# Another order for the first stage of a hybrid decoder block, and other PSUM banks for its first three projections

## The chip, the cores and the metric

The kernel runs on one core of a Trainium2 chip. The metric is the time of one execution on the device in microseconds, the median of three runs. The trace is that of one profiled execution. The engines are TensorE (PE, with its weight loads PEld), VectorE (DVE), ScalarE (ACT), GpSimd (POOL) and SyncE (SP), which issues the DMA transfers.

## The reference, cut to what matters

One decoder block over 512 tokens of 1024 values, all in float32:

```
h = RMSNorm(x)
P = h @ W_in            # q, k, v of two attentions, their branch gates, two merge gates
y_A = sliding-window attention with sinks(q, k, v) @ W_up_A
y_B = gated sum of compressed, selected and window attention @ W_up_B
x = x + (sigmoid(gA) * y_A + sigmoid(gB) * y_B) @ W_out
x = x + ConvFFN(RMSNorm(x));  out = RMSNorm(x)
```

## The kernel before, in words

Every float32 product is made of three matmuls of shorter operands: each matrix is split into a high part (rounded) and a low part (the rest), and high x high, high x low and low x high are summed in one PSUM bank (`three`, lines 108 to 112). The split is a cast on ScalarE (`split`, line 93) and a subtraction on VectorE or GpSimd (line 99).

The kernel has four stages. The first one takes `x` and the first weights and makes the values `v` and the first three projections. Attention follows, in units of one block of 128 queries and one group of heads; between the steps of a unit the later projections, the gates and the up-projections are issued as fillers, so that TensorE has work while the softmax runs on VectorE and ScalarE. Then come the output projection and the FFN with its convolution, which are nearly all matmuls.

The first stage is written as a list of short units, `FIRST` (lines 37 to 45), which are issued one by one in just that order (`do`, line 183) under a manual schedule: each engine executes its own units in the order of the list and waits at a unit whose inputs are not there. The units that matter here:

- `tpTH`: four transposes of token block T, half H of `x` into a bank of the tag `pt`; `xhTH` (ScalarE, line 207) and `xlTH` (VectorE, line 209) take the high and low part out of it, to `XH` and `XL`.
- `vTHCI`: two matmuls (line 237) of the values of token block T into the bank of `vT`. The banks are `mm`, `mm`, `o` and `sc` for T = 0 to 3. `vbT`, `vaT` (ScalarE) and `lbT`, `laT` (VectorE, line 183) read them when the sum is complete, `egT` and `gT` the gates.
- `ms`, `r` (GpSimd, line 217), `dg`, `rb`, `rs`: the reciprocal norms of the rows, and their copy over all columns.
- `jgJ` (VectorE, line 262), `jhJ` (ScalarE, line 265), `jlJ` (GpSimd, line 269): weight block J of the first three projections, scaled and split. J = 0, 1, 2 are `ka`, `qa0`, `qa1`.
- `pJK`: three matmuls of projection J, row block K, straight from `XH` and `XL`; `mJ` multiplies the result by the norms (line 277).
- `xaK` (GpSimd, line 283), `scK`, `yhK`, `ylK` (lines 285, 291, 293): the normalised `x`, which the later projections read as `xTh` and `xTl`.

PSUM has eight banks here, by tag: `mm` 2, `sc` 2, `pt` 3, `o` 1. A new tile of a tag takes the bank of the oldest one and so waits for the readers of it. Behind the list a scheduler orders the rest of the program on each engine by times that it works out itself, starting from the state in which the first stage leaves the engines; the first projection there is `kc`, whose result is cut into blocks (`cx`, line 390, and `XX0`) for the hidden layer `h1_00` (line 405).

Of the kernel before, what the change touches and what calls it, by code (L numbers as in the profile page):

```python
# [34 lines left out]


FIRST = '''
dum1 sq00 gt gc tp00 wh1 dum2 wh0 wl1 dum3 xh00 wl0 tp10 sq10 xl00 v0000 v0001 xh10 v0002 wh2 v1000 xl10 tp20 wh3 wl2
v1002 sq20 v1010 wl3 v0012 xh20 v1011 sq30 v0011 xl20 v2000 v2001 sq01 v2010 tp30 wh5 v0010 wh4 wl5 v1012 xh30 wl4
v1001 tp01 sq11 xl30 v3001 tp11 xa3 xh01 v3002 sq21 xl01 tp21 v0101 xh11 tc xa2 v0102 tp31 xh21 xl11 v1100 wh7 v1101  # L40
xl21 xa1 xh31 v1102 wl7 v0100 sq31 pg xl31 wh6 xa0 ms jg0 v1110 pgc r v0112 wl6 v1112 xa4 v3100 dg v0111 jh0 nr v1111
jg1 v0110 xa6 eg1 v2110 vb1 v2111 eg0 g1 vb0 rb jh1 g0 jl0 v3111 lb0 v2011 rs lb1 v2002 jg2 va1 v2100 va0 v2012 v2102
v2112 sc3 jh2 v2101 jl1 sc0 v3012 v3011 eg2 sc2 yh0 v3101 g2 v3010 vb2 v3110 va2 la0 yh3 v3000 la2 v3102 la1 yh2 v3112
yl3 jl2 p04 lb2 eg3 vb3 g3 p00 va3 la3 p02 lb3 sc6 p07 yl0 yh6 p01 xa7 yl2 p06 yl6 p05 xa5 sc7 p03 sc1 yh7 p22 sc4 yh1
p20 sc5 yh4 m0 p23 yh5 yl7 p26 yl5 p24 yl1 p25 yl4 p27 p21 p11 m2 p17 p16 p14 p13 p15 p10 p12 m1'''
NPA, NPB = (1, 2, 3), (2, 3)
BANKS = dict(mm=2, sc=2, pt=3, o=1)
SPLIT, CUT = 3, 256
# [15 lines left out]
def hybrid(tc, x, wv, wblk, w1, w2, wua, wub, wout, wfi, wfo, nmix, nffn, nfin, sinks, par, table, onehot, out):  # L64
# [9 lines left out]
    with es:  # L74
# [9 lines left out]
        def slot(i, shape, dt, name):  # L84
            return SL.tile(shape, dt, tag=f"s{i}", name=name)

        def bank(tag, name):
            return PS.tile([P, 512], F32, tag=tag, name=name, bufs=BANKS[tag])

        f = lambda t: t.bitcast(F32)  # L90
# [18 lines left out]
        def three(ps, wh, wl, xh, xl, start, stop):  # L109
            T.matmul(ps, wh, xh, start=start, stop=False)  # L110
            T.matmul(ps, wh, xl, start=False, stop=False)  # L111
            T.matmul(ps, wl, xh, start=False, stop=stop)  # L112
# [25 lines left out]
        def rstd_of(ssq, name):  # L138
            r = SM.tile([P, 1], F32, tag="rstd", bufs=3, name=f"rstd_{name}")
            V.tensor_scalar(r, ssq, 1.0 / D, EPS, op0=ALU.mult, op1=ALU.add)  # L140
            G.tensor_tensor(r, r, mhalf, op=ALU.pow)
            return r
# [22 lines left out]
        diag, rs = (AT.tile([P, S], F32, tag=g, name=n) for g, n in (("ptl", "diag"), ("pth", "rs")))  # L165
        scale, rstd, nrstd, *sq2 = (SM.tile([P, NT], F32, tag=g, name=g + "x", bufs=2) for g in ("nma", "sma", "nmb", "smb", "nmc"))
        first = FIRST.split()
        ps_v, out_v, tp_x, psj, raws, hls, sums, pgs_t, tot, last_of = {}, {}, {}, {}, {}, {}, {}, [], [], {}
        early = AORD.split()[:3]
# [3 lines left out]
        def out_of(t):  # L173
            if t not in out_v:
                ps = ps_v[t][:, 0:384].rearrange("p (n d) -> p n d", d=64)
                out_v[t] = ps[:, 0:2], ps[:, 2:6], SM.tile([P, 24], F32, tag="eg", name=f"eg{t}", bufs=2)
            return out_v[t]

        def values(dst, t, part, hi):
            if hi:  # L180
                A.mul(dst[:, t, :, 0:64], part, rstd[:, t : t + 1])
            else:
                V.scalar_tensor_tensor(dst[:, t, :, 64:128], part, rstd[:, t : t + 1], f(dst[:, t, :, 0:64]), op0=ALU.mult, op1=ALU.subtract)

        def do(u):
# [44 lines left out]
            elif what == "wl":  # L230
                V.scalar_tensor_tensor(xu(wvl, n[0]), xu(wvr, n[0]), gcol[:, n[0] : n[0] + 1], f(xu(wvh, n[0])), op0=ALU.mult, op1=ALU.subtract)
            elif what == "v":
                t, h, c, i = n
                if t not in ps_v:
                    ps_v[t] = bank(("mm", "mm", "o", "sc")[t], f"v{t}")
                for k in range(4 * h + 2 * c, 4 * h + 2 * c + 2):
                    T.matmul(ps_v[t][:, :NV], xu((XH, XH, XL)[i], k)[:, t * P : (t + 1) * P], xu((wvh, wvl, wvh)[i], k),
                             start=(u == mine[0] and k % 2 == 0), stop=(u == mine[-1] and k % 2 == 1))
            elif what in ("va", "la"):
                values(VA, n[0], out_of(n[0])[0], what == "va")  # L240
            elif what in ("vb", "lb"):
                values(VB, n[0], out_of(n[0])[1], what == "vb")
            elif what == "eg":
                A.activation(out_of(n[0])[2], ps_v[n[0]][:, 384:408], AF.Exp, scale=nrstd[:, n[0] : n[0] + 1])
            elif what == "g":
                t, eg = n[0], out_of(n[0])[2]
                V.tensor_scalar(eg, eg, 1.0, None, op0=ALU.add)
                V.reciprocal(gate[:, t].rearrange("p a h -> p h a"), eg.rearrange("p (h a) -> p h a", a=3))
                if t == 0:
                    V.tensor_scalar(gate[:, 0, 0], gate[:, 0, 0], valid0, None, op0=ALU.mult)  # L250
            elif what == "tc":
                V.tensor_copy(tabc, tab.rearrange("p (b h) -> p b h", b=2)[:, :, None].to_broadcast([33, 2, 16, 8]))
            elif what == "pg":
                pgs_t.extend(bank("pt", f"pg{i}") for i in range(2))
                for c0, c1, b, i, d0 in pgs:
                    T.matmul(pgs_t[i][:, d0 : d0 + c1 - c0], tabc[:, b].rearrange("p c h -> p (c h)"), oh[:, c0:c1], start=True, stop=True)
            elif what == "pgc":
                for c0, c1, b, i, d0 in pgs:
                    A.copy(gsb[:, c0:c1], pgs_t[i][:, d0 : d0 + c1 - c0])
            elif what == "jg":  # L260
                w = raws[n[0]].rearrange("p (k q) -> p k q", k=KD)
                V.tensor_tensor(w, w, gcol[:, :, None].to_broadcast([P, KD, P]), op=ALU.mult)
            elif what == "jh":
                hls[n[0]] = WR.tile([P, 2, 1024], F32R, tag="hl", name=f"hl_{early[n[0]]}", bufs=3)
                A.copy(hls[n[0]][:, 0], raws[n[0]])
            elif what == "jl":
                for c in range(0, 1024, 256):
                    cs = slice(c, c + 256)
                    G.tensor_tensor(hls[n[0]][:, 1, cs], raws[n[0]][:, cs], f(hls[n[0]])[:, 0, cs], op=ALU.subtract)
            elif what == "p":  # L270
                j, k = n
                if j not in psj:
                    psj[j] = bank(("mm", "mm", "sc")[j], f"p_{early[j]}")
                ks = slice(k * P, (k + 1) * P)
                three(psj[j], hls[j][:, 0, ks], hls[j][:, 1, ks], xu(XH, k), xu(XL, k), u == mine[0], u == mine[-1])
            elif what == "m":
                V.tensor_tensor(psj[n[0]], psj[n[0]], rs, op=ALU.mult)
            elif what == "xa":
                k = n[0]
                sums[k] = AT.tile([P, S], F32, tag="P", name=f"xa{k}", bufs=8)  # L280
                for c in range(0, S, 256):
                    cs = slice(c, c + 256)
                    G.tensor_tensor(sums[k][:, cs], f(xu(XH, k))[:, cs], f(xu(XL, k))[:, cs], op=ALU.add)
            elif what == "sc":
                V.scalar_tensor_tensor(sums[n[0]], sums[n[0]], gcol[:, n[0] : n[0] + 1], rs, op0=ALU.mult, op1=ALU.mult)
            elif what in ("yh", "yl"):
                if not xTh:
                    xTh.extend(slot(h, [P, 4, S], F32R, f"xTh{h}") for h in range(2))
                    xTl.extend(slot(2 + h, [P, 4, S], F32R, f"xTl{h}") for h in range(2))
# [523 lines left out]
        for mp in range(4):  # L813
            hl = weight(wub[mp], f"up1_{mp}", G if mp in U1J else None)
            for mm in range(2):
# [6 lines left out]
                gt = GB[m // 4][:, m % 4]  # L822
# [24 lines left out]
        for t in range(NT):  # L847
# [14 lines left out]
            r = rstd_of(ssq, f"n2_{t}")  # L862
# [43 lines left out]
        for h in range(2):  # L906
# [10 lines left out]
            for t in range(NT):  # L917
# [91 lines left out]
```

## Time and profile before

| | us |
|---|---|
| median of three runs | 758.54 |
| the runs | 758.47 to 760.33 |
| the profiled execution | 759.33 |
| its span | 757.5 |

The span is what the engines' instructions cover; the execution's own time is 1.8 us longer. In the rows below a line of a timeline is: start, duration of the group, engine, line of the kernel, operation, output<-inputs, shapes, count; in brackets the idle time of the engine ahead of it and what the profile thinks ended it. Numbers of tiles are left out there (`hl_qa` is that of `qa0`, `qa1` and others).

### The profile page before, as it was taken

To read this page: it belongs to the slowest core of one execution; us is meant where nothing else is said; L and a number is where in the kernel's file an instruction comes from. 1 tells how busy PE (TensorE), PEld (TensorE's weight loads), DVE (VectorE), ACT (ScalarE), POOL (GpSimd) and SP (SyncE) were. 2 spreads that over 40 slices of the span, in tenths; PEclk is the share of its full clock that TensorE was granted. 3 is DMA by queue.
4 is the path that set the end of the run, shared out by engine and by line. 5 is a ranking of instruction groups with operands and counts; after the bars stand their busy time and mean duration, and the time that the engine had idled before them with its cause. 6 is when DMAs were issued, how large, how long until landed. Compare 5 with 4: busy or idle time off the path is not lost.

```text
span 757.5 us, 9971 instructions
## 1 busy us (share of the span) xinstructions
PE 741.2 (98%) x3600; PEld 621.3 (82%) x3600; DVE 447.5 (59%) x915; ACT 375.6 (50%) x699; POOL 198.1 (26%) x275
## 2 busy tenths in 40 slices
PE   9899999999999999999999999999999999999996
PEld 7788887788888888878899888888888888888885
DVE  5987888457554667857466565556556654214223
ACT  7556778555657674664245344434444443113213
POOL 3973867425442554407200000000000000002001
PEclk9999999999999999999999999999999999999999
DMA  8353356221111211406222322222232324323202
GB/s 309 126 127 112 111 165 171 84 83 58 56 57 57 83 57 56 141 28 199 79 84 84 105 91 98 97 96 100 89 106 88 106 88 135 104 91 98 97 29 111
DMA packets 26029, 76.75 MB, mean 101 GB/s; under 512 B 3923, under 2 KB 6107, under 8 KB 25980
## 3 DMA queue, kind: packets, MB, share of 16 engines
q1 hardware_dynamic: 25964, 76.12, 30.9%
q8 instruction: 28, 0.46, 0.2%
q14 instruction: 21, 0.17, 0.1%
q10 hardware_dynamic: 16, 0.00, 0.0%
HBM read 72.96 MB, written 3.15 MB: 100 GB/s over the span
## 4 chain that ended last, share of the span: by engine, by line
PE 86%; DVE 5%; ACT 4%; issue 2%; POOL 1%; DMA 1%; SPq 0%; POOLq 0%; ACTq 0%; DVEq 0%
PE ug L112 11%; PE ug L110 11%; PE ug L111 11%; PE fo L902 5%; PE fo L904 5%; PE fo L903 5%; PE pT L592 2%; PE up L110 2%; PE p_ga L111 2%; PE p_ga L110 2%; PE up L112 2%; PE p_ga L112 2%; PE up L111 2%; PE wo L112 2%; PE wo L110 2%; PE wo L111 2%
## 5 line engine op out<-in xcount | busy, mean ns | idle before, releaser
L111 PE MATMUL ug<-hTl,hl_fi 128*128 128x512 f32 (+1 forms) x376 | 141.1, 375 | 0.0
L112 PE MATMUL ug<-hTh,hl_fi 128*128 128x512 f32 (+1 forms) x376 | 141.1, 375 | 0.0
L110 PE MATMUL ug<-hTh,hl_fi 128*128 128x512 f32 (+1 forms) x376 | 140.9, 376 | 0.0
L928 POOL TENSOR_TENSOR X<-X,nfin 128x512 f32<-128x512 f32 x4 | 5.2, 1314 | 296.9 <-ACT junk L926 296.9
L885 ACT ACTIVATE cv<-ug,prm 128x512 f32<-128x512 f32 x44 | 34.4, 781 | 96.2 <-PE ug L112 96.2
L111 PEld LDWEIGHTS ug<-hTl,hl_fi 128*128 128x128 f32 x376 | 70.8, 188 | 12.9
L112 PEld LDWEIGHTS ug<-hTh,hl_fi 128*128 128x128 f32 x376 | 70.8, 188 | 12.7
L110 PEld LDWEIGHTS ug<-hTh,hl_fi 128*128 128x128 f32 x376 | 70.6, 188 | 12.7
L886 DVE SCALAR_TENSOR_TENSOR cv<-ug,prm,cv 128x511 f32<-128x511 f32 x44 | 33.0, 750 | 77.0 <-ACT cv L885 76.9
L903 PE MATMUL fo<-hl_fo,AH 128*128 128x512 f32 x176 | 68.5, 389 | 0.0
L902 PE MATMUL fo<-hl_fo,AH 128*128 128x512 f32 x176 | 67.3, 389 | 0.0
L99 DVE TENSOR_TENSOR hl_fo<-raw_fo,hl_fo 128x1024 fp32r<-128x1024 f32 x22 | 27.1, 1234 | 64.6 <-ACT hl_fo L93 64.6
L93 ACT CAST hl_fo<-raw_fo 128x1024 fp32r<-128x1024 f32 x22 | 23.1, 1052 | 65.7 <-PE fo L904 65.7
L99 DVE TENSOR_TENSOR hl_fi<-raw_fi,hl_fi 128x1024 fp32r<-128x1024 f32 x44 | 53.5, 1217 | 0.8 <-ACT hl_fi L93 0.8
L904 PE MATMUL fo<-hl_fo,AL 128*128 128x512 f32 x128 | 49.8, 389 | 0.0
L522 ACT ACTIVATE Pb<-Pb,nmb 128x512 f32<-128x512 f32 (+3 forms) x64 | 35.9, 562 | 27.5 <-DVE nmb L585 26.1
L93 ACT CAST hl_fi<-raw_fi 128x1024 fp32r<-128x1024 f32 x44 | 45.6, 1039 | 1.5 <-PE wo L112 1.5
L99 DVE TENSOR_TENSOR ptl<-pT,pth 128x512 fp32r<-128x512 f32 x54 | 36.5, 684 | 15.0 <-ACT pth L93 11.3
L93 ACT CAST pth<-pT 128x512 fp32r<-128x512 f32 x54 | 30.8, 585 | 22.4 <-PE pT L592 14.6
L585 DVE CUSTOM_DVE_ANT_0 Pb<-scores,TB 128x512 f32<-128x512 f32 (+3 forms) x64 | 30.6, 485 | 16.8 <-PE scores L581 15.7
L902 PEld LDWEIGHTS fo<-hl_fo,AH 128*128 128x128 f32 x176 | 33.0, 188 | 6.9
L903 PEld LDWEIGHTS fo<-hl_fo,AH 128*128 128x128 f32 x176 | 33.0, 188 | 6.9
(335 smaller groups left out, 1769.4 us busy)
## 6 DMA issues: line engine op xcount, KB each, us to landing
raw_fi<-in_wfi_dram SPq DMA_DIRECT2D x44, 512.0 KB, 3.2
raw_fo<-in_wfo_dram SPq DMA_DIRECT2D x22, 512.0 KB, 3.2
raw_w<-in_w_dram SPq DMA_DIRECT2D x8, 512.0 KB, 3.3
raw_ga<-in_wblk_dram SPq DMA_DIRECT2D x8, 512.0 KB, 3.5
raw_gb<-in_wblk_dram SPq DMA_DIRECT2D x8, 512.0 KB, 3.3
raw_wo<-in_wout_dram SPq DMA_DIRECT2D x5, 512.0 KB, 4.1
x<-in_x_dram SPq DMA_DIRECT2D x8, 256.0 KB, 5.7
raw_qa<-in_wblk_dram SPq DMA_DIRECT2D x4, 512.0 KB, 5.0
```

The costliest lines, as they stand in the source:

```text
L93: A.copy(hi, src)
L99: (eng or V).tensor_tensor(lo[sl], src[sl], f(hi)[sl], op=ALU.subtract)
L110: T.matmul(ps, wh, xh, start=start, stop=False)
L111: T.matmul(ps, wh, xl, start=False, stop=False)
L112: T.matmul(ps, wl, xh, start=False, stop=stop)
L522: last_exp[0] = A.activation(a[0], a[1], AF.Exp, **k)
L585: V.tensor_tensor_reduce(ptile[:, :n], ps[:, :n], Tt[:, h, y0 : y0 + n], 1.0, HUGE, ALU.add, ALU.min, nm)
L885: A.activation(c, ps, AF.Identity, scale=cw(2, blk), bias=cb(blk))
L886: V.scalar_tensor_tensor(c[:, 1:], ps[:, : S - 1], cw(1, blk), c[:, 1:], op0=ALU.mult, op1=ALU.add)
L902: T.matmul(po[t], ah, wh, start=(k == 0), stop=False)
L903: T.matmul(po[t], ah, wl, start=False, stop=False)
L904: T.matmul(po[t], al, wh, start=False, stop=(k == NF - 1))
```

## The change

The list `FIRST` is replaced by another order of the same units, and the banks of the three projections `p` now have the tag `pt` in place of `mm`, `mm` and `sc`:

```diff
 FIRST = '''
-dum1 sq00 gt gc tp00 wh1 dum2 wh0 wl1 dum3 xh00 wl0 tp10 sq10 xl00 v0000 v0001 xh10 v0002 wh2 v1000 xl10 tp20 wh3 wl2
...
+dum1 sq00 gt gc tp00 wh1 dum2 xh00 wl1 dum3 wh0 xl00 tp10 sq10 v0000 wl0 v0002 wh2 v0001 wh3 wl2 tp20 sq20 v0010 wl3
...
             elif what == "p":
                 j, k = n
                 if j not in psj:
-                    psj[j] = bank(("mm", "mm", "sc")[j], f"p_{early[j]}")
+                    psj[j] = bank("pt", f"p_{early[j]}")
```

TensorE around the first product of `p_ka`, before: all of `v` is done when it comes (`v3_247` is the bank of `v3`).

```order
L237 MATMUL v3_247<-wvl1_85,XH1_91 128x408 x2
L237 MATMUL v3_247<-wvh0_82,XH0_90 128x408 x2
L237 MATMUL v3_247<-wvh1_83,XH1_91 128x408 x2
L237 MATMUL v3_247<-wvh0_82,XH0_90 128x408 x2
L237 MATMUL v3_247<-wvh1_83,XL1_93 128x408 x4
L110 MATMUL p_ka_434<-XH1_91,hl_ka_332 128x512
L111 MATMUL p_ka_434<-XL1_93,hl_ka_332 128x512
```

The same place now:

```order
L237 MATMUL v2_227<-wvl1_85,XH1_91 128x408 x2
L237 MATMUL v3_231<-wvl0_84,XH0_90 128x408 x2
L237 MATMUL v3_231<-wvh0_82,XH0_90 128x408 x2
L225 MATMUL rb_366<-diag_97,VA_95 128x512
L110 MATMUL p_ka_376<-XH1_91,hl_ka_321 128x512
L111 MATMUL p_ka_376<-XL1_93,hl_ka_321 128x512
```

And TensorE in the third projection of the list, `p_qa0`, now:

```order
L110 MATMUL p_qa0_467<-XH1_91,hl_qa0_345 128x512
L111 MATMUL p_qa0_467<-XL1_93,hl_qa0_345 128x512
L112 MATMUL p_qa0_467<-XH1_91,hl_qa0_345 128x512
L237 MATMUL v2_227<-wvh1_83,XH1_91 128x408 x2
L110 MATMUL p_qa0_467<-XH1_91,hl_qa0_345 128x512
L111 MATMUL p_qa0_467<-XL1_93,hl_qa0_345 128x512
L112 MATMUL p_qa0_467<-XH1_91,hl_qa0_345 128x512
L237 MATMUL v3_231<-wvh1_83,XL1_93 128x408 x2
L237 MATMUL v2_227<-wvh0_82,XL0_92 128x408 x2
```

The last products of `v2` and `v3`, ten pairs, moved from ahead of the first projection into the third; `rb` stands right ahead of `p_ka`.

VectorE ahead of and at the blocks of `p_kc`, which the hidden layer `h1_00` reads as `XX0`, before:

```order
L467 SCALAR_TENSOR_TENSOR QA0_559<-p_qa1_482,QA0_559 64x512
L467 SCALAR_TENSOR_TENSOR QA0_559<-p_qa0_517,QA0_559 64x512
L390 TENSOR_TENSOR cx_545<-p_kc_609,prm_88 64x8x31 x3
L585 ISA Pa_588,nma_586<-scores_589,TA_575 128x130
L585 ISA nma_586 128x1
L390 TENSOR_TENSOR cx_545<-p_kc_609,prm_88 64x8x31 x2
L585 ISA Pa_613,nma_586<-scores_614,TA_575 128x130
L585 ISA nma_586 128x1
L390 TENSOR_TENSOR cx_545<-p_kc_609,prm_88 64x8x31 x3
L99 TENSOR_TENSOR XX0_687<-cx_545,XX0_687 128x16x62
```

The same place now:

```order
L183 SCALAR_TENSOR_TENSOR VA_95<-v2_227,smax_100,VA_95 128x2x64
L183 SCALAR_TENSOR_TENSOR VB_89<-v2_227,smax_100,VB_89 128x4x64
L183 SCALAR_TENSOR_TENSOR VB_89<-v3_231,smax_100,VB_89 128x4x64
L277 TENSOR_TENSOR p_qa0_467<-p_qa0_467,rs_98 128x512
L457 TENSOR_TENSOR KA_549<-p_ka_376,KA_549 64x4x128
L458 TENSOR_TENSOR KA_549<-p_ka_376,KA_549 64x4x128
L467 SCALAR_TENSOR_TENSOR QA0_559<-p_qa1_428,QA0_559 64x512
L467 SCALAR_TENSOR_TENSOR QA0_559<-p_qa0_467,QA0_559 64x512
L390 TENSOR_TENSOR cx_545<-p_kc_609,prm_88 64x8x31 x8
L467 SCALAR_TENSOR_TENSOR QA0_559<-p_qa0_467,QA0_559 64x512
L99 TENSOR_TENSOR XX0_687<-cx_545,XX0_687 128x16x62
```

The first reductions of `scores` moved behind `XX0`, and the last readers of `v2` and `v3` (`VA`, `VB`) moved to just ahead of it. On TensorE the two first pairs of `scores` moved likewise, from between `p_kc` and `p_qa2` to behind both.

TensorE near the end of attention, from the fourth pair of `scores` of a window unit (`scores_3413` is the first of the next unit's; `ob` is an attention output, `up0` and `up1` are fillers), before:

```order
L580 MATMUL scores_3413<-KS_1281,QB1_1971 128x160
L581 MATMUL scores_3413<-KS_1281,QB1_1971 128x160
L110 MATMUL up0_6_3399<-YA1_1057,hl_up0_3_3327 128x512
L111 MATMUL up0_6_3399<-YA1_1057,hl_up0_3_3327 128x512
L112 MATMUL up0_6_3399<-YA1_1057,hl_up0_3_3327 128x512
L739 MATMUL ob_3276<-pch_3283,VZ_547 128x128
L739 MATMUL ob_3276<-pcl_3284,VZ_547 128x128
```

The same place now:

```order
L111 MATMUL up1_3_3676<-YB0_1985,hl_up1_1_3653 128x512
L112 MATMUL up1_3_3676<-YB0_1985,hl_up1_1_3653 128x512
L580 MATMUL scores_3413<-KS_1281,QB1_1971 128x160
L581 MATMUL scores_3413<-KS_1281,QB1_1971 128x160
L592 MATMUL pT_3374<-ident_87,Pb_3107 128x128
L592 MATMUL pT_3374<-ident_87,Pb_3136 128x128
L592 MATMUL pT_3374<-ident_87,Pb_3173 128x128
L592 MATMUL pT_3374<-ident_87,Pb_3205 128x128
L580 MATMUL scores_3444<-KS_1281,QB1_1971 128x160
```

The end of `up0_6`, all of `up0_7` and the first six matmuls of `up1_3` moved ahead of `scores_3413`.

## Rows read from the trace of the kernel before

**Rows 1.** The page: busy time and instructions by engine, clock by slices.
```profile
PE 741.2 (98%) x3600; PEld 621.3 (82%) x3600; DVE 447.5 (59%) x915; ACT 375.6 (50%) x699; POOL 198.1 (26%) x275
...
PEclk9999999999999999999999999999999999999999
```

**Rows 2.** TensorE's waits at 0-60, 60-160, 300-420 us: us, times, longest.
```profile
PE p_ka L110 <- ACT xTh L291: 2.8, 1, 2.8
...
PE scores L580 <- DVE nma L585: 1.0, 2, 0.7
...
PE p_qb L110 <- ACT cx L409: 0.6, 1, 0.6
...
PE p_ksl L110 <- DVE cx L390: 0.2, 1, 0.2
...
PE up L110 <- DVE oy L606: 1.6, 1, 1.6
PE up L110 <- DVE nmb L585: 0.2, 1, 0.2
```

**Rows 3.** Busy time by engine from 130 to 300 us (length, then each engine, clock).
```profile
130.00:300.00 170.00, 169.78 (x882) 142.50 (x881) 102.06 (x332) 103.54 (x229) 76.14 (x107) 1.00 0.19 63
```

**Rows 4.** Timeline of TensorE around the first projection.
```profile
29.32 1.28 PE L237 MATMUL v<-wvh,XH 128*128 128x408 f32 x6
30.44 0.91 PE L237 MATMUL v<-wvh,XL 128*128 128x408 f32 x4
34.13 0.76 PE L110 MATMUL p_ka<-XH,hl_ka 128*128 128x512 f32 x1 [2.79 <-ACT xTh L291]
...
37.53 0.40 PE L112 MATMUL p_ka<-XH,hl_ka 128*128 128x512 f32 x1
...
41.17 0.39 PE L110 MATMUL p_qa<-XH,hl_qa 128*128 128x512 f32 x1
```

**Rows 5.** Busy time in stretches: length, PE, PEld, DVE, ACT, POOL, granted clock.
```profile
30.00:40.00 10.00, 7.21 (x27) 5.76 (x26) 9.93 (x19) 4.40 (x11) 10.00 (x12) 0.83 0.69 173
...
20.00:56.34 36.34, 33.55 (x147) 28.27 (x146) 33.52 (x52) 20.20 (x38) 31.57 (x39) 0.95 0.47 131
```

**Rows 6.** Timeline of VectorE: the readers of `v` ahead of `p_ka`.
```profile
33.73 0.77 DVE L183 SCALAR_TENSOR_TENSOR VA<-v,smax,VA 128x128 fp32r<-128x128 f32 x3
```

**Rows 7.** Timeline of GpSimd behind `r`.
```profile
20.02 1.95 POOL L217 TENSOR_TENSOR smax<-nmax,warm 128x4 f32<-128x4 f32 x1
21.94 4.32 POOL L283 TENSOR_TENSOR xa<-XH,XL 128x256 f32<-128x256 f32 x4
26.22 3.81 POOL L269 TENSOR_TENSOR hl_ka<-raw_ka,hl_ka 128x256 fp32r<-128x256 f32 x4
...
37.31 4.62 POOL L283 TENSOR_TENSOR xa<-XH,XL 128x256 f32<-128x256 f32 x4
...
46.21 3.96 POOL L99 TENSOR_TENSOR hl_kc<-raw_kc,hl_kc 128x256 fp32r<-128x256 f32 x4 [1.56 <-issue]
50.13 2.83 POOL L99 TENSOR_TENSOR hl_qa<-raw_qa,hl_qa 128x256 fp32r<-128x256 f32 x4
```

**Rows 8.** Timeline of TensorE: the start of `p_kc`.
```profile
52.05 0.39 PE L110 MATMUL p_kc<-xTh,hl_kc 128*128 128x512 f32 x1
```

**Rows 9.** The blocks of `p_kc` (line 390, durations in ns), their cast and low part.
```profile
L390 DVE TENSOR_TENSOR cx<-p_kc,prm x8: 399/411/419, 57.7 to 61.2; 64x248 f32<-64x248 f32 x8
...
61.63 1.03 ACT L93 CAST XX<-cx 128x992 fp32r<-128x992 f32 x1 [0.72 <-DVE cx L390]
...
62.69 1.19 DVE L99 TENSOR_TENSOR XX<-cx,XX 128x992 fp32r<-128x992 f32 x1 [1.10 <-ACT XX L93]
```

**Rows 10.** Busy time from `scores_3413` to `up1_1`: all engines, then line 536 alone (VectorE).
```profile
305.41:318.15 12.74, 12.47 (x75) 10.45 (x73) 10.13 (x41) 7.10 (x22) 8.09 (x12) 1.00 0.63 197
...
305.41:318.15 12.74, 1.36 (x2) 1.00 0.63 197
```

**Rows 11.** Timeline of TensorE: the wait for the last attention output.
```profile
328.38 0.47 PE L110 MATMUL up<-YB,hl_up 128*128 128x512 f32 x1 [1.65 <-DVE oy L606]
```

More of the change, by code (lines that the diff above doesn't have):

```diff
@@ L37 @@
 FIRST = '''
-dum1 sq00 gt gc tp00 wh1 dum2 wh0 wl1 dum3 xh00 wl0 tp10 sq10 xl00 v0000 v0001 xh10 v0002 wh2 v1000 xl10 tp20 wh3 wl2
[L39 to L45, printed above, removed]
+dum1 sq00 gt gc tp00 wh1 dum2 xh00 wl1 dum3 wh0 xl00 tp10 sq10 v0000 wl0 v0002 wh2 v0001 wh3 wl2 tp20 sq20 v0010 wl3
+v0012 xh10 tp30 v0011 sq30 xl10 v1011 v1000 xh30 v1002 v1001 xh20 xl30 v1010 wh5 v2000 xl20 v3002 wh4 v2001 wl5 xa3
+sq01 v2010 wl4 v3000 wh6 tp01 v1012 sq11 wl6 tp11 xa0 v2012 xh01 tp21 tc sq21 v0101 v0100 xl01 xh11 xa1 v2011 v3012
+xh21 xl11 v1100 wh7 v1101 xl21 v0102 sq31 v0110 xa2 jg0 v1110 tp31 v1102 wl7 xh31 pg jh0 ms jg1 r v0111 pgc v3111 jl0
+v2111 dg v0112 v1112 jh1 nr v1111 xl31 v2112 eg1 jg2 v2101 eg0 v3001 vb0 v3010 vb1 rb g0 va0 xa6 va1 p04 lb0 jh2 la0
+p03 la1 lb1 rs jl2 p00 g1 p02 sc2 p07 p01 sc0 yh2 p05 sc3 yh0 p06 xa5 yl2 yh3 p22 p26 yl3 p23 jl1 sc6 p24 yl0 yh6 p25
+p21 yl6 p27 m0 p20 xa4 sc5 p17 m2 yh5 v2100 p14 sc1 xa7 v3102 v2002 yl5 yh1 v2110 v3100 yl1 p16 v3101 sc7 v3110 v3112
+sc4 yh7 p12 v3011 yl7 yh4 p13 va3 yl4 v2102 eg3 vb3 p11 la3 vb2 p15 g3 eg2 va2 p10 g2 la2 lb2 lb3 m1'''
 NPA, NPB = (1, 2, 3), (2, 3)
```

## The prediction

> **What bounds the kernel now.** I read the page first: TensorE is busy 741.2 us [rows 1] of a span of 757.5 us. Whatever an edit does elsewhere counts only where TensorE waits, or where its clock falls. So the second view was the list of what TensorE waited for, by stretches [rows 2]. Up to 60 us there is one wait in the middle, 2.8 us before the first projection `p_ka`; from 60 to 160 us there are some 3 us in small waits on VectorE and ScalarE; from 300 to 420 us there are 1.8 us, of which 1.6 us stand where the last attention output is awaited. From 130 to 300 us it hardly waits at all: 169.78 us busy of 170 [rows 3].
>
> Third, the timeline of TensorE around the wait in the middle [rows 4]. The last product of `v` ends at 31.35 us and `p_ka` begins at 34.13 us. After the wait the matmuls start 0.43 us apart (eight of them from 34.13 to 37.53 us) and from there 0.2275 us apart (16 of them from 37.53 to 41.17 us). The stretch 30 to 40 us has a granted clock of 0.83 [rows 5]: TensorE ran at the lower of its levels, 1.2 GHz, after that idle time. It cost 3.40 us for what takes 8 x 0.2275 = 1.82 us at 2.4 GHz, so 1.58 us more. The idle times of 1.65 us and less [rows 2, 11] show no such fall, the clock stays at 9 tenths or more in all 40 slices of the page [rows 1].
>
> What ended the wait is named ScalarE's `xTh`. By the program it was another thing: `p_ka` takes the bank of `v0`, and the last reader of `v0` is VectorE's `la0`, first of three on line 183 that start at 33.73 us [rows 6]. It ends just ahead of 34.13. It stands late in VectorE's queue, which was busy 33.52 of the 36.34 us from 20 us on [rows 5].
>
> **The change part by part.** The units are the same; none is added or dropped. What differs is the order, and the banks of `p`.
>
> *The wait before `p_ka`.* The bank of `p_ka` is now one of the transposes', whose last reader is `xl31`. In the new order that stands a few units before, well ahead of `la0`. Ten pairs of `v` products (0.37 us a pair, three from 29.32 to 30.44 us) now stand behind the first projections, so `p_ka` comes up at about 31.35 - 3.7 = 27.6 us. It needs `hl_ka`, whose high part needs `jg0` and `jh0` alone and whose low part is GpSimd's first work behind `r` (end 21.97 us, then 3.81 us, so 25.8 us [rows 7]). So the whole 2.79 us goes, and with it the fall of the clock: 2.79 + 1.58 = 4.37 us. What is late next is GpSimd: `jl0`, `xa6`, `jl2`, `xa5`, `jl1` behind `r` are 3 x 3.81 + 2 x 2.16 = 15.75 us by [rows 7], so 37.7 us; the first product of `p_qa0`, 16 units of 0.68 us behind the start of `p_ka`, is at 27.6 + 10.9 = 38.5 us. I count no wait there, with 0.8 us to spare.
>
> *The place behind `p_kc`.* With 4.37 us gained `p_kc` starts at 52.05 - 4.37 = 47.68 us [rows 8]. In the new order `p_kc` and `p_qa2` come in a piece, 48 matmuls or 10.92 us, then two short pairs of `scores` (130 columns, an estimated 0.3 us by their share of 512), then `h1_00`: TensorE is there at 58.9 us. `h1_00` needs `XX0`, and VectorE's queue has to come through: its work of 33.52 us from 20 us on [rows 5], then the eight blocks of `cx` (0.41 us each, 3.3 us), ScalarE's cast (1.03 us) and the low part (1.19 us) [rows 9], so 20 + 33.52 + 3.3 + 1.03 + 1.19 = 59.0 us if VectorE never waits. It waited 2.8 us in that time before (36.34 - 33.52), and with all of that it would be 61.8 us. The wait is between 0.1 and 2.9 us; I take 1.0, nearer to the low end, since part of the waits before were for projections that now come earlier.
>
> *From 60 to 95 us.* The waits there are VectorE's and ScalarE's pace: 1.0 us for `nma` and 0.6 and 0.2 us for `cx` [rows 2]. A TensorE that arrives earlier waits longer for the same readers. Between 0 and as much again (1.8 us), I take 0.6.
>
> *The end of attention.* The scheduler places everything behind the first stage, and starting from another state it places the fillers otherwise. In the old order 21 filler matmuls (three of `up0_6`, twelve of `up0_7`, six of `up1_3`) stand between `scores_3413` and `up1_1`; in the new order none, they all stand ahead. The old stretch lasted from 305.41 to 318.15 us, 12.74 us. Without the fillers (21 x 0.2275 = 4.78 us) and without the 0.3 us that TensorE waited, its own work there is 7.66 us. VectorE was busy 10.13 us there, of which 1.36 us are products of gates (line 536) that go ahead with the fillers [rows 10]: 8.77 us remain. So TensorE waits at least 1.1 us, were VectorE packed without a gap, and 3.7 us if VectorE keeps the 2.6 us of gaps it had. I take 2.2. The 1.65 us at the very end [rows 11] I leave as they are.
>
> The sum: 4.37 - 1.0 - 0.6 - 2.2 = 0.57 us gained. The profiled execution took 759.33 us (its span of 757.5 and 1.8 around it), which gives 758.8. The median of the runs is 758.54, 0.8 below the profiled one, which gives 758.0. By the bounds the terms reach from 4.37 - 0.1 - 1.1 = 3.2 us gained to 4.37 - 2.9 - 1.8 - 3.7 = 4.0 us lost; they will not all be at one end, and the forecast's own range is 756.3 to 760.2.
>
> **The rivals.**
>
> *The gain is kept.* The softmax at the end may be packed well enough that TensorE's lead simply moves everything forward, as the stretch without waits from 130 to 300 us suggests [rows 3]. For it: VectorE too starts the later stages earlier, and ScalarE is busy only 7.10 of the 12.74 us [rows 10]. Against it: with no filler in that stretch TensorE has less to do (7.66 us) than VectorE (8.77 us). Time: 758.54 - 4.37 + 0.3 for a small wait at `h1_00`, 754.5 us.
>
> *The end of attention eats more than the lead.* One place, the stretch from `scores_3413` to `up1_1`: if the fillers hid all they covered, their 4.78 us turn into waiting. Then 4.37 - 1.0 - 0.6 - 4.78 = -2.0, so 760.5 us; and if one of these idle times is as long as the 2.79 us of [rows 4] the clock falls once more and 1.58 us come on top, 762.1 us. I put it at 761.3. It decides from 2.8 us of waiting there, where the lead is used up, and is slower by more than a measurement can tell from 5.0 us. For it: 2.6 us of gaps in VectorE in the same stretch. Against it: 0.8 us of them were waits for fillers that now come first.
>
> *GpSimd becomes the bound of the first stage.* The new order has its chain from `r` to `jl1` with hardly a gap, beside VectorE's products of two inputs. In the trace the low part of a block costs 3.96 us on GpSimd while VectorE works on such products and 2.83 us a little later [rows 7], and the halves of `xa` cost 1.155 us (4 in 4.62 us) at their longest. Sixteen pieces at 1.155 us are 18.5 us and end at 40.5 us, 2.0 us behind what `p_qa0` needs. Time: 758.0 + 2.0 = 760.0 us. The Trainium skill, page "GPSIMD Engine Reference", section "1. Specifications", states that GpSimd shares its SBUF interfaces with VectorE and contends with VectorE instructions that have two SBUF inputs. By that rule the denser order would be paid for on GpSimd; the trace agrees in direction, 3.96 against 2.83 us for the same work.
>
> *The change doesn't do what it says.* `p_ka` could wait as long as before, on another reader of the transposes' banks (`pgc` for the two next) or on `hl_ka`. Against it: these end by 26 us by the rows above. Then no lead arises, and only the worse placed end counts: 758.54 + 1.1 = 759.6 us.
>
> **How the numbers follow.** About 0.3%, 2.3 us, is what a measurement of this kernel can tell from no change: faster is below 756.3, slower above 760.8. The forecast (758.0) has 0.56, the gain kept 0.19, the eaten lead 0.14, GpSimd 0.06, no effect 0.05. Faster: 0.18 of the second case and 0.05 of the first, 0.23. Slower: 0.10 of the third, 0.02 of the first and 0.03 of GpSimd's, together 0.15. The rest, 0.62, is no change. The range leaves out half of the kept gain and most of the eaten lead, 0.18 in all: 754.6 to 760.9 us.
>
> **What would show it.** In the changed kernel's trace: the timeline of TensorE has no idle time before `p_ka`, products of `v` between those of `p_qa`, and no granted clock below 1.00 before 100 us; `p_kc` starts near 47.7 us (wrong if later than 49.5). TensorE waits for `XX` before `h` near 59 us, about 1 us. Between 300 and 320 us the list of waits names VectorE's `nmb`, `Pb` or `ptl` with some 2 us in total, where before it named 0.2 us; if these are under 0.7 us, the gain is kept and the forecast is wrong; if they are over 4 us, the third case holds.

## The result, and the profile after

The changed kernel takes 768.7 us in the median of four runs (765.9 to 770.8), the kernel before 759.0 beside it: the ratio is 1.0121 (interval 1.0102 to 1.0140), so it is slower by 1.2%. The forecast was 758.0 with a range of 754.6 to 760.9. The profiled execution took 765.93 us (span 764.1), the shortest of the four; it is 6.6 us above that of before (759.33), and that is what the rows below account for. The median lies another 2.8 us higher; what that may be is read in experiment 5.

TensorE's timeline in the first stage, after (columns as in the rows of before):

```profile
26.83 0.79 PE L110 MATMUL p_ka<-XH,hl_ka 128*128 128x512 f32 x1
...
39.73 0.50 PE L112 MATMUL p_qa<-XH,hl_qa 128*128 128x512 f32 x1 [0.96 <-POOL hl_qa L269]
...
48.56 0.39 PE L110 MATMUL p_kc<-xTh,hl_kc 128*128 128x512 f32 x1
...
61.90 0.30 PE L580 MATMUL scores<-KA,QA 128*128 128x130 f32 x1 [2.12 <-DVE QA L467]
...
63.46 1.47 PE L405 MATMUL h<-hl_w,XX 128*128 128x256 f32 x8 [1.15 <-DVE XX L99]
...
66.10 0.58 PE L580 MATMUL scores<-KA,QA 128*128 128x258 f32 x1 [0.43 <-DVE nma L585]
...
66.70 0.63 PE L110 MATMUL p_qa<-xTh,hl_qa 128*128 128x512 f32 x1
67.12 0.63 PE L111 MATMUL p_qa<-xTl,hl_qa 128*128 128x512 f32 x1
```

The 2.79 us before `p_ka` [rows 4] are gone: `p_ka` comes at 26.83 us without a wait, products of `v` stand inside `p_qa`, and `p_kc` begins at 48.56 us, 3.49 us earlier than before [rows 8]. Then the lead vanishes. `h` (the hidden layer `h1_00`) begins at 63.46 us, and before it had begun at 64.03. TensorE stands idle for 2.12 + 1.15 + 0.43 = 3.70 us within 6.5 us, each time until VectorE is done, and behind that its matmuls start 0.43 us apart. The stretches (length, PE, PEld, DVE, ACT, POOL, granted clock, DMA share, GB/s) say how long:

```profile
60.00:64.00 4.00, 0.95 (x6) 0.87 (x7) 3.53 (x10) 2.86 (x5) 0.00 (x0) 1.00 0.42 131
64.00:68.00 4.00, 3.57 (x16) 3.09 (x15) 3.91 (x10) 3.77 (x13) 0.00 (x0) 0.52 0.26 79
68.00:72.00 4.00, 4.00 (x13) 3.12 (x12) 1.21 (x3) 0.09 (x1) 1.12 (x3) 0.62 0.49 183
```

A granted clock of 0.52 and 0.62 over 4 us each means 4 x 0.48 + 4 x 0.38 = 3.4 us lost at 1.2 GHz, twice what the fall of before cost [rows 5]. In the first of these stretches TensorE is busy 0.95 of 4 us and VectorE 3.53.

What VectorE waited for from 20 to 64 us (us in total, times, longest), before, and then after:

```profile
DVE cx L390 <- PE p_kc L112: 1.3, 1, 1.3
...
DVE p_qa L277 <- PE p_qa L112: 0.8, 1, 0.8
...
DVE KA L457 <- ACT KA L456: 0.6, 1, 0.6
```

```profile
DVE KA L457 <- ACT KA L456: 2.3, 1, 2.3
DVE diag L221 <- POOL smax L217: 0.9, 1, 0.9
```

Before, VectorE waited for TensorE (1.3 and 0.8 us). After, it waits for TensorE no more, and still the low part of `XX0` ends only 0.56 us earlier (63.32 us, before 63.88 [rows 9]): VectorE's own work of 38.7 us from 20 to 63.3 us (next row), with 4.6 us in which it stands idle, sets the end of the stage. Its waits that the profile names sum to 4.9 us before and still to 4.1 us after, now all for ScalarE and GpSimd.

```profile
20.00:63.32 43.32, 39.22 (x177) 32.22 (x175) 38.68 (x63) 23.90 (x43) 33.48 (x43) 1.00 0.43 134
```

TensorE's waits from 60 to 160 us and from 305 to 346 us, after, against [rows 2] and two more lines of before, which stand first:

```profile
PE h L405 <- DVE QB L467: 0.7, 1, 0.7
...
PE oa L646 <- DVE oy L606: 0.5, 1, 0.5
```

```profile
PE scores L580 <- DVE QA L467: 2.1, 1, 2.1
PE scores L580 <- DVE nma L585: 1.4, 2, 1.0
PE p_ksl L110 <- DVE cx L390: 1.2, 1, 1.2
PE h L405 <- DVE XX L99: 1.1, 1, 1.1
PE p_qb L110 <- ACT cx L409: 1.1, 1, 1.1
...
PE up L110 <- DVE oy L606: 1.7, 1, 1.7
PE ob L743 <- DVE ptl L99: 0.7, 3, 0.3
PE pT L592 <- DVE Pb L732: 0.3, 1, 0.3
PE scores L580 <- DVE nmb L585: 0.2, 1, 0.2
```

From 60 to 160 us the waits sum to 6.9 us, where before they were 3.0. The end of attention is read from the stretch between `scores_3413` and the first `wo` (line 110 of the output projection), before and after:

```profile
305.41:338.93 33.52, 31.61 (x166) 26.21 (x164) 22.15 (x68) 20.32 (x46) 9.04 (x14) 1.00 0.27 86
```

```profile
314.11:345.46 31.35, 28.12 (x144) 22.32 (x143) 21.32 (x67) 19.54 (x46) 6.33 (x10) 1.00 0.16 56
```

21 fillers of 0.2275 us left it, so it should have lasted 33.52 - 4.78 = 28.74 us; it lasted 31.35, 2.6 us more.

The sum: 2.79 + 1.7 (the old fall, 0.17 of 10 us in [rows 5]) gained, against 0.96 (`hl_qa`), 3.9 (waits of 60 to 160 us, 6.9 - 3.0), 3.4 (clock) and 2.6 (end of attention): 6.4 us lost of the 6.6 measured. This sum counts where TensorE stood or ran slowly; it doesn't yet say what caused each term.

### The profile page after: what moved, and what is told of

Same layout as the page of the kernel before. It is cut to its first block, busy times and chain, and to the rows that moved or that the text cites. A ratio compares the mean times of both kernels' runs of the same rounds, so it can differ in the third digit from the quotient of the medians.

```text
span 764.1 us, 9969 instructions
## 1 busy us (share of the span) xinstructions
PE 744.1 (97%) x3600; PEld 622.5 (81%) x3600; DVE 448.1 (59%) x915; ACT 374.6 (49%) x699; POOL 196.4 (26%) x275
## 4 chain that ended last, share of the span: by engine, by line
PE 87%; DVE 7%; ACT 3%; issue 2%; DMA 1%; POOL 1%; POOLq 0%; ACTq 0%; DVEq 0%
PE ug L112 10%; PE ug L110 10%; PE ug L111 10%; PE fo L902 5%; PE fo L904 5%; PE fo L903 5%; PE pT L592 3%; PE p_ga L110 2%; PE up L110 2%; PE p_ga L112 2%; PE p_ga L111 2%; PE up L111 2%; PE up L112 2%; PE wo L111 2%; PE wo L112 2%; PE wo L110 2%
```

## The experiments

Theory A, formed on these rows: VectorE's queue sets when `h1_00` can begin and again when `p_ksl` can; what TensorE gains ahead of them turns into idle time, and the clock falls on top. Theory B has any earlier TensorE punished by a worse order behind the first stage, theory C blames the banks, and theory D GpSimd. The rivals' forecasts stand in the expectations. Times are compared with runs of the kernel before on the same chip (medians 759.1 to 759.5). The profiled executions differ by some tenths of a us in when `p_ka` can start, so close comparisons are counted from there. The numbers are those of the expectations; there is no tenth.

**Experiment 1**, the old order with the new banks:

```diff
-                    psj[j] = bank(("mm", "mm", "sc")[j], f"p_{early[j]}")
+                    psj[j] = bank("pt", f"p_{early[j]}")
```

> The old order of the first stage, with only the banks of the three projections taken from the new version. Theory A (VectorE's queue sets when the hidden layer h1_00 can begin; in the old order it has about 3.5 us of slack between 50 and 58 us, in the new one none): the wait before p_ka (2.8 us) and the clock fall behind it (1.6 us) go, p_kc starts near 47.7 us, h1_00 moves from 64.0 to 60.5-62 us, and the kernel is 1.5 to 3.5 us faster than before (755 to 757). Theory B (any earlier TensorE is punished, because the order behind the first stage comes out worse): no faster than before, 758.5 to 762, with the loss between 300 and 340 us.

Measured: 759.9 us, ratio 1.0008 (0.9999 to 1.0017): no change. `p_ka` begins at 31.15 us, `p_kc` at 47.5 and `h1_00` at 60.37, 3.7 us earlier than before, as theory A expected. Then (TensorE's timeline, and the stretches around it):

```profile
83.27 0.47 PE L110 MATMUL p_ksl<-xTh,hl_ksl 128*128 128x512 f32 x1 [2.21 <-DVE cx L390]
```

```profile
80.00:84.00 4.00, 1.79 (x7) 1.22 (x8) 3.86 (x13) 2.77 (x5) 3.74 (x6) 1.00 0.00 0
84.00:88.00 4.00, 4.00 (x12) 3.10 (x12) 3.96 (x7) 1.58 (x6) 4.00 (x6) 0.58 0.41 131
```

VectorE is packed (3.86 of 4 us), TensorE waits 2.21 us for its blocks of `p_vc`, and loses 1.7 us more at the lower clock. The mechanism of theory A holds; its expected gain does not, because the next place of the same kind takes it.

**Experiment 2**, the new order with the old banks (the same two lines the other way round):

> The new order, with the banks of before. Theory A: TensorE waits about 2.3 us before p_ka (for the readers of v0) and about 4 us before p_kc (for the readers of p_ka), but VectorE is no later than in the new version, so h1_00 begins at 64 to 66 us with little wait of its own; total 764 to 769, within 3 us of the new version: the banks move the wait and do not make it. Theory C (the banks cause the loss, by holding the transposes' banks): as fast as before, 757 to 760.

Measured: 769.6 us, ratio 1.0146 (1.0125 to 1.0167). TensorE waits 1.3 us before `p_ka`, and then:

```profile
PE p_kc L110 <- DVE KA L458: 7.7, 1, 7.7
```

`p_kc` needs the bank of `p_ka`, whose readers in VectorE's queue come late. Theory C falls: without the new banks the new order is no better. The wait was longer than I expected and `h1_00` later (71.3 us). With experiment 1 all four pairs are measured: the old order takes 759.0 us with the old banks and 759.9 with the new ones, the new order 769.6 and 768.7. The order costs some 9 us with either banks, and the banks alone next to nothing.

**Experiment 3**, the kernel before with matmuls of no use in its idle time:

```diff
-yl3 jl2 p04 lb2 eg3 vb3 g3 p00 va3 la3 p02 lb3 sc6 p07 yl0 yh6 p01 xa7 yl2 p06 yl6 p05 xa5 sc7 p03 sc1 yh7 p22 sc4 yh1
+yl3 jl2 dum4 p04 lb2 eg3 vb3 g3 p00 va3 la3 p02 lb3 sc6 p07 yl0 yh6 p01 xa7 yl2 p06 yl6 p05 xa5 sc7 p03 sc1 yh7 p22 sc4 yh1
...
-                for i in range((6, 2, 3)[n[0] - 1]):
-                    T.matmul(bank("mm", "idle"), one[:, :P], one, start=True, stop=True)
+                for i in range((6, 2, 3, 9)[n[0] - 1]):
+                    T.matmul(bank("mm", "idle"), one[:, :P], one, start=True, stop=True) if n[0] < 4 else T.matmul(bank("pt", "warm"), xu(XH, 0)[:, :P], xu(XH, 0), start=True, stop=True)
```

> The kernel before, with 9 matmuls of no use (2.05 us, into a free bank) in its 2.8 us wait ahead of p_ka. If the fall of the clock comes from the idle time and costs 1.58 us: granted clock 1.00 from 30 to 40 us, p_kc starts 1.6 us earlier (near 50.4), and the kernel is 1.0 to 1.6 us faster (757.0 to 757.6). If the lead is lost at the next wait: the clock is 1.00 and the time is that of before within 0.4 us.

Measured: 759.1 us, ratio 1.0000 (0.9991 to 1.0008). The granted clock and the next waits:

```profile
30.00:40.00 10.00, 9.28 (x43) 7.52 (x42) 9.93 (x20) 4.19 (x11) 10.00 (x11) 1.00 0.72 174
```

```profile
PE p_kc L110 <- DVE KA L458: 0.9, 1, 0.9
```

The fall of the clock is gone, so it did come from the idle time. Of the 1.6 us that this gives, 0.9 go at once into a new wait for VectorE's readers of `p_ka`, and the time does not change. A clock that was kept up was worth nothing here, where VectorE set the pace.

**Experiment 4**, the same in the new version, behind the first scores:

```diff
-            ps = bank("sc", "scores")
+            ps = bank("sc", "scores"); [T.matmul(ps, Q[:, 0, :P], Kt[:, 0, 0, :512], start=True, stop=True) for _ in range(9 * (Tt is TA and (b, g, r) == (0, 0, 1)))]
```

> The new version, with 9 matmuls of no use (2.05 us, into the bank of the second scores) between the first and the second scores near 59.7 us, where TensorE waits 2.1 us for QA0. If the idle time there brings the clock fall of 6.8 us at half speed (3.4 us lost): the clock stays at 1.00 until 100 us, h1_00 still begins at 63.5 us, and the time falls by 3 to 3.5 us, to 763 to 765.5, with less scatter from run to run. If the clock fall has another cause: it stays, and the time is that of the new version, 766 to 771.

Measured: 765.8 us (765.4 to 765.9), ratio 1.0086. The scatter is gone and the median is 2.9 us lower; it is that of the new version's shortest run. I had expected 763 to 765.5 us and a clock of 1.00, and missed both. The matmuls of no use run from 59.40 to 61.70 us; timeline of TensorE behind them, and stretches:

```profile
63.18 1.19 PE L405 MATMUL h<-hl_w,XX 128*128 128x256 f32 x8 [1.21 <-DVE XX L99]
...
65.61 0.33 PE L580 MATMUL scores<-KA,QA 128*128 128x130 f32 x1 [1.06 <-DVE nma L585]
```

```profile
64.00:68.00 4.00, 2.65 (x12) 2.08 (x11) 3.27 (x10) 2.98 (x8) 0.00 (x0) 0.81 0.38 130
68.00:72.00 4.00, 4.00 (x15) 3.19 (x14) 1.30 (x3) 0.20 (x2) 1.12 (x3) 0.76 0.36 132
```

The two idle times that are left (1.21 and 1.06 us) still brought a fall, half as long as before: 4 x 0.19 + 4 x 0.24 = 1.7 us. So 1.7 us were won there, and `p_ksl` began only 0.5 us earlier (59.8 us behind the start of `p_ka`, in the new version 60.3). Between the two profiled executions, 765.71 and 765.93 us, little is left of it. That VectorE took it back fits the wait for `cx` at `p_ksl`, which stays 1.2 us.

**Experiment 5**, the diagonal on ScalarE:

```diff
-                V.tensor_tensor(diag.rearrange("p (t q) -> p t q", t=NT), ident[:, None, :].to_broadcast([P, NT, P]),
-                                rstd[:, :, None].to_broadcast([P, NT, P]), op=ALU.mult)
+                for t in range(NT):
+                    A.mul(diag[:, t * P : (t + 1) * P], ident, rstd[:, t : t + 1])
```

> The new version with one VectorE work of 1.22 us ahead of the chain taken off it: the diagonal matrix (line 221) is made by four instructions on ScalarE. Theory A (VectorE's queue from 28 to 61 us sets the start of h1_00): cx starts 1.2 us earlier (56.8 instead of 58.0), h1_00 at 62.2 instead of 63.4, idle time near 60 us 1.2 us shorter, total 1 to 3 us less than the new version. Theory D (GpSimd's halves set it, as the wait of 1 us for hl_qa suggests): h1_00 stays within 0.3 us of 63.4 and the total is that of the new version.

Measured: 766.0 us (765.5 to 769.8), ratio 1.0096. A miss: `cx` began at 58.4 us and `h1_00` at 63.8, which is 36.6 us behind `p_ka` as in the new version. The 1.22 us were taken off VectorE ahead of a place where it then waited 1.3 us for ScalarE's `eg`, which now stood behind the diagonal. So the result, which is the one that theory D forecast, does not speak for GpSimd either: the relief never reached the place that it was meant for. The profiled execution was one of 769.82 us and shows what the longer runs have (timeline, then a stretch):

```profile
335.54 0.76 PE L110 MATMUL up<-YB,hl_up 128*128 128x512 f32 x1 [1.70 <-DVE oy L606]
```

```profile
330.00:345.00 15.00, 12.98 (x47) 9.80 (x47) 4.81 (x9) 8.79 (x15) 0.00 (x0) 0.77 0.00 0
```

Behind the last attention output the clock falls here too: 15 x 0.23 = 3.5 us. The same wait of 1.7 us brings no fall in the profiled execution of the new version, nor in that of before [rows 11]. That the new version's own long runs have this fall is likely from their mean granted clock (0.988 and 0.989, against 0.993 in the profiled one), but no profile of one of them shows it.

**Experiments 6 and 7**, the low part of one later weight block (`h1_01`) on GpSimd, with the old order and new banks (6), and in the kernel before (7):

```diff
-POOLJ = set('ga0 ga1 ga2 ga3 ga4 ga5 ga6 ga7 gb0 gb1 gb2 gb3 gb4 gb6 gb7 h00 h02 h10 h12 h13 ka kc ksl qa2 qa3 qb0 qb1 qb2'.split())
+POOLJ = set('h01 ga0 ga1 ga2 ga3 ga4 ga5 ga6 ga7 gb0 gb1 gb2 gb3 gb4 gb6 gb7 h00 h02 h10 h12 h13 ka kc ksl qa2 qa3 qb0 qb1 qb2'.split())
```

> The old order with the new banks, and the low part of one later weight block (h1_01's, 1.22 us on VectorE near 64 us) moved to GpSimd, which is idle there. Theory A: the lead of 3.4 us, which experiment 1 lost at 83 us to the wait of p_ksl for VectorE's blocks of p_vc (2.2 us), to the scores ahead of it (1.3 us) and to the clock fall behind (1.7 us), is now lost by 1.2 us less of waiting and without the clock fall: 756.0 to 757.5, faster than before. If the lead is lost to something else than VectorE's load: 759 to 760, as in experiment 1.

> The kernel before, with the same low part on GpSimd: VectorE is relieved but TensorE has no lead to keep. Theory A: within 0.7 us of before (the waits of 60 to 95 us are 1.8 us in all and only part of them can go). If that low part is by itself what matters: as much faster as experiment 6.

Measured: 755.6 us in experiment 6, ratio 0.9952 (0.9938 to 0.9966), and 759.5 in experiment 7, ratio 1.0001 (0.9992 to 1.0010). Of TensorE's waits of 60 to 160 us in experiment 6, the one at `p_ksl`:

```profile
PE p_ksl L110 <- DVE cx L390: 0.4, 1, 0.4
```

1.22 us less on VectorE turn the wait of 2.2 us at `p_ksl` into 0.4, the clock stays up (1.00 from 60 to 100 us), and the lead is kept to the end. Without the lead the same edit is worth nothing. Both are as theory A has it, and experiment 6 gained a little more than expected.

**Experiment 8**, the new version with the same edit:

> The new version with the same low part on GpSimd. On the first stage it does nothing (h1_00 at 63.4 us, clock fall behind it as before), but the order that comes out for the end of attention has the fillers between scores_3413 and up1_1 again. If the fillers' places cost the 2.6 us at 300 to 340 us: these come back, the excess there is 3.1 us as before instead of 5.8, and the total is 2.5 to 4 us below the new version (763 to 766). If the end of attention waits for VectorE whatever stands there: 766 to 770.

Measured: 762.1 us (762.0 to 762.8), ratio 1.0037 (1.0025 to 1.0049). `h1_00` stays late, but the fillers stand between `scores_3413` and `up1_1` again, and the stretch to the first `wo`, from 307.87 to 341.35 us, lasts 33.48 us, as before (33.52), with the same two waits. The row is of a window of that length 0.27 us later:

```profile
308.14:341.62 33.48, 31.56 (x165) 26.18 (x165) 22.15 (x68) 20.40 (x44) 8.78 (x14) 1.00 0.27 90
```

So the 2.6 us at the end of attention come from where the fillers stand. The total is lower than I expected: the profiled execution is 3.9 us below that of the new version, of which 0.7 lie ahead of `p_ka` (26.13 us, in the new version 26.83) and 2.6 here. The runs scatter by 0.8 us only; but so do the four of experiment 4, by 0.5 us, with the fillers of the new version, so that it isn't shown that the scatter comes from the fillers.

**Experiment 9**, the scalings of `xa` ahead of the low parts of `xT`, in the new version (`m2` moves behind them too):

```diff
-p21 yl6 p27 m0 p20 xa4 sc5 p17 m2 yh5 v2100 p14 sc1 xa7 v3102 v2002 yl5 yh1 v2110 v3100 yl1 p16 v3101 sc7 v3110 v3112
-sc4 yh7 p12 v3011 yl7 yh4 p13 va3 yl4 v2102 eg3 vb3 p11 la3 vb2 p15 g3 eg2 va2 p10 g2 la2 lb2 lb3 m1'''
+p21 yl6 p27 m0 p20 xa4 sc5 p17 yh5 v2100 p14 sc1 xa7 v3102 v2002 yh1 v2110 v3100 sc4 p16 v3101 yh4 sc7 m2 v3110 v3112
+yl5 yh7 p12 v3011 yl1 yl4 p13 va3 yl7 v2102 eg3 vb3 p11 la3 vb2 p15 g3 eg2 va2 p10 g2 la2 lb2 lb3 m1'''
```

> The new version with its last VectorE units in another order: the scalings of the last three xa (line 285) come ahead of the four low parts of xT (line 293) instead of between them. KA lies in the memory of gx, which these scalings read, so ScalarE's casts to KA can begin only behind the last of them; in the new version VectorE then has nothing to do for 2.26 us (47.3 to 49.55 us). Theory A: that gap falls to under 1 us, cx starts 1.5 to 2 us earlier, h1_00 at 61.5 to 62 us instead of 63.4, and with the shorter idle time of TensorE the clock falls less: 762.5 to 765.5. If the gap only moves (VectorE waits for GpSimd's last xa or for ScalarE instead): h1_00 at 63 us or later, 765.5 to 769.

Measured: 765.6 us (764.6 to 766.0), ratio 1.0078. VectorE's waits from 20 to 64 us:

```profile
DVE XX L99 <- ACT XX L93: 0.8, 1, 0.8
DVE xa L285 <- POOL xa L283: 0.6, 1, 0.6
DVE eg L247 <- ACT eg L244: 0.5, 1, 0.5
...
DVE KA L457 <- ACT KA L456: 0.2, 1, 0.2
```

The wait for `KA` fell from 2.3 to 0.2 us and came back in pieces, for GpSimd, ScalarE and the cast of `XX0`; `h1_00` began at 63.8 us (36.4 us behind `p_ka`, in the new version 36.6). The gap only moved: the 2.3 us were not the cause by themselves.

**Experiment 11**, experiment 6 with the low parts of the first three weight blocks on VectorE:

```diff
-                for c in range(0, 1024, 256):
-                    cs = slice(c, c + 256)
-                    G.tensor_tensor(hls[n[0]][:, 1, cs], raws[n[0]][:, cs], f(hls[n[0]])[:, 0, cs], op=ALU.subtract)
+                for c in range(0, 1024, 1024):
+                    cs = slice(c, c + 1024)
+                    V.tensor_tensor(hls[n[0]][:, 1, cs], raws[n[0]][:, cs], f(hls[n[0]])[:, 0, cs], op=ALU.subtract)
```

> The version of experiment 6 with the low parts of the first three weight blocks (line 269) on VectorE, in three instructions of 1024 columns, instead of twelve of 256 on GpSimd. If GpSimd's work beside it makes VectorE's two-input instructions slower (line 285 took 0.74 us without GpSimd beside it and 1.22 us with it, line 293 0.68 and 1.23): six or more of the sixteen get back 0.5 us each, which pays most of the 3 x 1.22 us added, h1_00 is 0 to 1.5 us later than in experiment 6, and the total 755.5 to 757. If the longer times have nothing to do with GpSimd: lines 285 and 293 keep their 15.5 us in sum, h1_00 is 3 to 4 us later, and the lead is lost: 757.5 to 760.

Measured: 754.5 us, ratio 0.9937 (0.9923 to 0.9950), the fastest version here and faster than I expected. VectorE's groups from 20 to 64 us in experiment 6, and in this one (busy us, mean ns):

```profile
L285 DVE SCALAR_TENSOR_TENSOR xa<-xa,gx,rs 128x512 f32<-128x512 f32 x8 | 7.7, 1015 | 0.0
L293 DVE TENSOR_TENSOR xTl<-xa,xTh 128x512 fp32r<-128x512 f32 x8 | 7.0, 919 | 0.0
```

```profile
L285 DVE SCALAR_TENSOR_TENSOR xa<-xa,gx,rs 128x512 f32<-128x512 f32 x8 | 6.1, 805 | 0.0
L293 DVE TENSOR_TENSOR xTl<-xa,xTh 128x512 fp32r<-128x512 f32 x8 | 5.1, 686 | 0.0
...
L269 DVE TENSOR_TENSOR hl_qa<-raw_qa,hl_qa 128x1024 fp32r<-128x1024 f32 x2 | 2.4, 1215 | 0.0
L269 DVE TENSOR_TENSOR hl_ka<-raw_ka,hl_ka 128x1024 fp32r<-128x1024 f32 x1 | 1.2, 1212 | 0.0
```

VectorE took on 3.6 us and the sixteen instructions beside it became 3.5 us shorter; `h1_00` began 28.45 us behind `p_ka`, in experiment 6 29.22. (The profiled execution also began `p_ka` 0.76 us earlier than that of experiment 6.)

**Experiments 12 and 13**, the same edit in the new version (12), and experiment 11 with the old banks (13):

> The new version with the low parts of the first three weight blocks (line 269) on VectorE instead of GpSimd (as in experiment 11, but in the new order and without the other edit). Theory A with contention (in the new order lines 285 and 293 take 16.9 us in sum beside GpSimd, without it about 12): VectorE has 3.64 us more and 5 us less to do, the wait of 1 us for hl_qa goes, h1_00 moves from 37.1 us behind rb to 35.5-36.5 us, the idle time near 60 us falls from 3.7 to 2-3 us and with it part of the clock fall, and at the end of attention the fillers stand as before (2.6 us less there): 758.5 to 763. If the new order loses for another reason than VectorE's load: 765 to 769.

> Experiment 11 without the new banks: old order, old banks, both reliefs of VectorE (low part of h1_01 on GpSimd, low parts of line 269 on VectorE). If the banks give the lead and the relief only lets it be kept: TensorE waits 2.8 to 3.9 us before p_ka again, with the clock fall, and the kernel is within 1 us of before (758.5 to 760.5). If the relief alone is what made experiment 11 faster: 754.5 to 757.

Measured: 759.9 us in experiment 12, ratio 1.0007 (0.9998 to 1.0017), and 760.4 in experiment 13, ratio 1.0021 (1.0012 to 1.0030). TensorE's timeline in experiment 12, with its clock, and the wait of experiment 13:

```profile
59.28 0.30 PE L580 MATMUL scores<-KA,QA 128*128 128x130 f32 x1 [0.99 <-DVE QA L467]
...
61.28 1.18 PE L405 MATMUL h<-hl_w,XX 128*128 128x256 f32 x8 [0.76 <-DVE XX L99]
...
63.83 0.80 PE L110 MATMUL p_qa<-xTh,hl_qa 128*128 128x512 f32 x1 [0.56 <-ACT cx L409]
```

```profile
60.00:70.00 10.00, 8.59 (x30) 6.90 (x31) 6.49 (x17) 5.69 (x17) 2.01 (x3) 0.66 0.42 149
```

```profile
34.13 0.47 PE L110 MATMUL p_ka<-XH,hl_ka 128*128 128x512 f32 x1 [3.50 <-ACT VA L181]
```

Relieved, the new version comes back by 8.8 us to the time of before (6.0 us against its shortest run). The low parts cost VectorE 3.8 us, and the sixteen instructions of lines 285 and 293 took 11.4 us in place of 16.4; `h1_00` is 1.9 us earlier, counted from `p_ka`, and the fillers stand as before (33.50 us from `scores_3413` to `wo`). The profiled execution, 761.94 us, is the longest of the eleven; it still loses 3.4 us at the lower clock there, while the others have a mean granted clock of 0.993 to 0.997 against its 0.990. It is 4.0 us below the profiled execution of the new version, of which 2.6 are the end of attention and 1.0 the wait for `hl_qa`, which is gone. What the earlier `h1_00` brought by itself is therefore not shown, nor does this edit separate a relief of VectorE from one of GpSimd, which lost twelve pieces by it. Without the new banks the relief gives nothing, because the wait before `p_ka` stays. The gain of experiment 11 takes both: in the old order the banks make the lead, and the relief of VectorE lets it last.

## Why the prediction was wrong

*The wait before `p_ka` and its clock (4.37 us): right.* Both went, 2.79 and 1.7 us.

*No wait for GpSimd at `p_qa0`: a small miss.* I left 0.8 us to spare; TensorE waited 0.96 us. GpSimd ended `jl1` at 39.68 us and not at 37.7:

```profile
29.07 3.73 POOL L269 TENSOR_TENSOR hl_qa<-raw_qa,hl_qa 128x256 fp32r<-128x256 f32 x4 [1.06 <-ACT hl_qa L265]
```

It waited 1.06 us for ScalarE's cast ahead of `jl2`, which my sum did not have, and the four pieces of `jl0` and of `jl1` took 4.26 and 4.62 us and not 3.81, beside VectorE's work of two inputs. The rival on GpSimd had the slower pieces but not that wait, and a price of 2.0 us. The Trainium skill, page "SBUF — State Buffer", section "Who interferes with whom", goes further than the page I named: a VectorE instruction with two SBUF inputs and a GpSimd instruction that reads SBUF exclude one another, and whichever comes second waits. By that VectorE pays as well, which I did not price. The trace agrees in direction: line 285 takes 0.73 us at its shortest and 1.32 at its longest, and experiment 11 shortens it by taking work off GpSimd.

*The place behind `p_kc` (1.0 us, bounds 0.1 and 2.9): the step that failed.* `p_kc` itself came at 48.56 us, the forecast 47.7 and the wait for `hl_qa`, so the lead was there. The place cost 3.70 us of idle time and 3.4 us of clock. The sum of VectorE's work was right (38.0 us by my terms without the cast, 38.7 measured), but I let it stand 1.9 us in all (0.9, and 1.03 for the cast) where it stood 4.6, and I bounded that by the waits it had before. Those for TensorE did vanish. Others grew in their place, `KA`'s first, and in experiment 9, where the wait for `KA` was removed, others took it up. Why just these waits grew stays open. The other fault was the clock, which I had at nothing here: I counted its fall as a gain where an idle time went, and not as a price where the same idle time would come up again in one piece. With 7.1 us here in place of 1.0 the forecast becomes 764.1 us on the median's basis. That is 4.6 us short of the measured median: 1.0 of them is `hl_qa`, 0.4 the end of attention, and 2.8 is what the median has above the profiled execution.

*60 to 95 us (0.6 us): about right.* Apart from the place above, TensorE's waits of 60 to 160 us are 3.2 us, before 3.0.

*The end of attention (2.2 us): right in size,* 2.6 measured over the stretch to the first `wo`, and in experiment 8 it goes when the fillers stand as before. The waits that were to show it, for `nmb`, `Pb` and `ptl`, come to 1.2 us and not to some 2; in the rest TensorE's matmuls only follow each other less closely (28.12 us busy where 31.61 - 4.78 = 26.83 were to be expected). What I did not see is that in some executions the clock falls there as well (3.5 us in experiment 5).

*Which rival came true?* None as written. The eaten lead (761.3) had the right form, a lead that turns into waiting and then a fall of the clock, at the wrong place. I had given a slower kernel a chance of 0.15.

## What to carry to other kernels

When an edit gives one engine a lead, write down for each later meeting with the next busiest engine when that engine can be there at the earliest, from its own queue, and take the lead as lost at the first meeting where it is later. Where TensorE then has nothing to fill the wait, price the fall of its clock with it. A relief of the slower engine and a lead of the faster one can each be worth nothing alone (experiments 1, 7 and 13) and gain 3.8 to 4.8 us together (6 and 11): try them as a pair.

## What the runs showed of the hardware

A GpSimd that takes work off VectorE can cost it about as much as it saves: three low parts on VectorE (3.6 us) shortened sixteen neighbouring instructions by 3.5 us, while GpSimd's twelve pieces were gone (experiment 11 against 6).

The clock fell behind several short idle times as it does behind one long one: behind 1.21 and 1.06 us (experiment 4) and behind 0.99, 0.76 and 0.56 us (experiment 12), while the single one of 1.65 or 1.70 us at the end of attention brought no fall in thirteen profiled executions and a fall in one (experiment 5). Matmuls of no use kept the clock up (experiment 3), but gave no time there (759.1 us with and without).
